# A hybrid trunk layer on one core: where four kinds of loads are issued, where two sums of weights are kept, and which engine adds the last residual columns

## The chip, the cores and the metric

The kernel runs on 1 core of one Trainium2 chip. The metric is the device time of one execution in microseconds (us), taken as the median over runs. One profiled execution gives the trace from which the rows below are quoted. The engines are TensorE (PE, with PEld for its weight loads), VectorE (DVE), ScalarE (ACT), GpSimd (POOL) and SyncE (SP, which here only issues DMAs).

## The reference, cut to what matters

```python
h = concat([meta, x])                                   # 272 rows of 2048
proj = rmsnorm(h, norm_mix) @ w_in                      # q, k, v, gates of 8 retention and 4 mLSTM heads
...
mix = concat([ret, hm]) @ w_out
h = h + mix
u = rmsnorm(h, norm_ffn)
up = causal_dwconv(u @ w_up, ffn_conv_w, ffn_conv_b)    # 11264 columns, kernel of 3
gate, val = split(up, [5632])
h = h + (silu(gate) * val) @ w_down                     # 5632 x 2048
return rmsnorm(h, norm_final)[16:]                      # 256 x 2048
```

All of it is float32. The change touches the first projection (its loads), the product with `w_down` (its loads and two sums of weight blocks) and the last residual sum ahead of the final norm.

## The kernel before, in words

Every float32 product is made of three products of 128-row blocks: weights w are split into whi (ACT rounds w, a CAST row) and wlo = w - whi (DVE), activations likewise into xh and xl, and PE sums xh*whi, xl*whi and xh*wlo in a bank. So each weight tile takes a DMA into the ring `wraw` (4 buffers), a cast on ACT, a subtraction on DVE, and then matmuls. The rings `whi` and `wlo` have 5 buffers each.

**The ramp** (the loop at L207). The first projection runs over 16 blocks k of the contracted axis while they still arrive: a DMA of hT (the input, 128x272 for each k) and one of w0 (128x320 for each k: two weight tiles and the gate columns), in portions of k = 0, 1, and then pairs. SP issues them, but for the first two w0 loads, which ACT issues, and `par`, the column of norm factors. ACT makes xh of each k and casts each w0 portion to whi; DVE makes wlo, the low part of the gate columns (the 64 columns of whi written at L227) and xl. Ahead of it PE multiplies a tile of ones WARM times (L199, two rows in the trace for each).

**The up projection and the down products**, in two halves of the 5632 columns. Each half has 11 down steps q of 256 columns of w_down, and there are two passes b = 0 and b = 2 over pairs of 512 output columns, with two row tiles tt. Steps 0, 4, 9 and 10 are plain: two loads of 512 KB in `wraw`, each cast and subtracted, and 24 matmuls (`product`, L814). The other steps are fast (`seven`, L832): seven products in place of eight. A fast step reads two DMAs into one of the two buffers `left` (they lie in hT; `turn` alternates), `kept` (256 KB, a sum made earlier and stored to DRAM) and three blocks of `wd7` (768 KB). From these DVE makes the sums ta (128x1024, L844) and tb (128x512, L845), and ta and tb each take a buffer of the ring `wraw` too. In half 1, pass 2, steps run in the order 0, 1, 4, 2, 7, 3, 5, 6 and then plain ones.

After the last fast step `share` combines four banks of PSUM and adds them to hn by DMAs that accumulate (hn<-x, issued by POOL); after the last step ACT copies the four banks of cs to x (L951), and these go to hn likewise. The banks are then written by the next pass.

**The tail** (L961). What the last four steps (`alone`) give to columns 1536 to 2047 of row tile 1 is summed apart, in two halves of 256 columns: PE, then DVE adds the bank to hn (L900), ACT squares it and sums (L694), then the chain for the final norm (`finish`: ACT Ln and Exp, DVE), and DVE and ACT scale hn (DVE L723 and L721, the latter with the gain `gfin`; columns that lie ready earlier are multiplied with the gain by POOL, L698) and store.

**What sets the order.** The framework orders the instructions of each engine by its own estimate of when they can run. `tc.issue_after(x)` keeps an instruction behind x in that order without a wait between engines of its own. Each engine and each DMA queue works in its order. SP waits at a DMA until its buffer is free, and all later DMAs of SP wait behind it.

## Time and profile before

| what | value |
|---|---|
| median of 3 runs | 1207.33 us (1207.29 to 1207.91) |
| profiled execution | 1207.7 us, its span 1205.9 us |
| TensorE clock granted, mean | 0.999 |
| PE busy | 1194.6 us, 99% of the span, 8956 matmul rows |
| DVE, ACT, POOL busy | 971.5, 709.5 and 162.8 us |
| moved by DMA | 263.27 MB, 218 GB/s over the span |

Times in the trace are counted from the first instruction. A row of the timeline is: start, duration, engine, line of the program, operation, written tile and read tiles, shape, how many in a row, and in brackets the idle time before it with what ended it. A matmul row's duration overlaps the next row's; the distance of two starts is what a matmul costs in a dense stretch.

### The profile page before, as it was taken

Reading aid. Unit: us, or ns where it says so; the run is one execution under the profiler, and the core shown is the slowest. Engines: PE = TensorE matmul, PEld = TensorE weight load, DVE = VectorE, ACT = ScalarE, POOL = GpSimd, SP = SyncE. Lnnn points to the kernel's source line nnn. Section 1 sums busy time; section 2 is a strip of 40 time slices with the busy share of each in tenths; the row PEclk is TensorE's granted clock in tenths of the full one; section 3 lists DMA queues with packets and bytes.
Section 4 is the critical chain, followed back from the end, with each engine's and each line's share of the span. In section 5 each row is a group of like instructions: output and inputs, shape, how many; then the busy total and the mean of one; then the engine's idle time right before and its main releaser. Section 6 shows DMA issues by size and latency. Waiting matters only on the chain.

```text
span 1205.9 us, 22794 instructions
## 1 busy us (share of the span) xinstructions
PE 1194.6 (99%) x8956; PEld 1151.2 (95%) x8956; DVE 971.5 (81%) x1444; ACT 709.5 (59%) x963; POOL 162.8 (14%) x223
## 2 busy tenths in 40 slices
PE   9999999999999999999999999999999999999997
PEld 9999999999999999999999998878999999998886
DVE  8968788766775966789889879897788778789897
ACT  8747656655656646555555557664555555556664
POOL 0100001111110311021122100202022112100232
PEclk9999999999999999999999999999999999999999
DMA  8765555666565965766766834959787777755956
GB/s 278 269 212 164 170 184 170 197 183 192 169 192 165 349 200 175 252 220 212 253 219 214 279 117 175 278 177 276 284 251 255 223 240 249 261 176 211 274 181 186
DMA packets 83004, 263.27 MB, mean 218 GB/s; under 512 B 14672, under 2 KB 18896, under 8 KB 82768
## 3 DMA queue, kind: packets, MB, share of 16 engines
q1 hardware_dynamic: 71952, 223.85, 57.0%
q0 software_dynamic: 10368, 37.11, 10.1%
q8 instruction: 70, 1.15, 0.4%
q10 hardware_dynamic: 576, 0.85, 0.2%
q14 instruction: 38, 0.31, 0.1%
HBM read 243.42 MB, written 11.27 MB: 211 GB/s over the span
## 4 chain that ended last, share of the span: by engine, by line
PE 96%; DMA 2%; DVE 1%; ACT 0%; issue 0%; SPq 0%; DVEq 0%; ACTq 0%
PE mmps L130 26%; PE mmps L131 25%; PE mmps L133 25%; PE atps L827 2%; PE atps L828 2%; PE atps L830 2%; PE mmps L860 2%; PE mmps L862 2%; PE mmps L859 2%; PE atps L862 1%; PE atps L860 1%; PE atps L859 1%; DMA hn<-x 1%; PE atps L379 1%; DMA hT<-in_wd 1%; PE atps L371 0%
## 5 line engine op out<-in xcount | busy, mean ns | idle before, releaser
L121 ACT CAST whi<-wraw 128x1024 fp32r<-128x1024 f32 x352 | 369.3, 1050 | 342.0 <-PE mmps L131 228.7
L123 DVE TENSOR_TENSOR wlo<-wraw,whi 128x1024 fp32r<-128x1024 f32 x352 | 432.3, 1230 | 72.5 <-ACT whi L121 70.0
L130 PE MATMUL mmps<-uh,whi 128*128 128x258 f32 x1408 | 346.1, 283 | 0.0
L131 PE MATMUL mmps<-ul,whi 128*128 128x258 f32 x1408 | 346.0, 283 | 0.0
L130 PEld LDWEIGHTS mmps<-uh,whi 128*128 128x128 f32 x1408 | 267.6, 190 | 0.1
L131 PEld LDWEIGHTS mmps<-ul,whi 128*128 128x128 f32 x1408 | 267.1, 190 | 0.1
L130 PE MATMUL mmps<-xh,whi 128*128 128x272 f32 (+2 forms) x864 | 219.8, 288 | 0.0
L131 PE MATMUL mmps<-xl,whi 128*128 128x272 f32 (+2 forms) x864 | 218.3, 286 | 0.0
L133 PE MATMUL mmps<-uh,wlo 128*128 128x258 f32 x1408 | 196.5, 282 | 0.0
L133 PEld LDWEIGHTS mmps<-uh,wlo 128*128 128x128 f32 x1408 | 179.9, 189 | 0.0
L131 PEld LDWEIGHTS mmps<-xl,whi 128*128 128x128 f32 x864 | 162.8, 188 | 0.0
L130 PEld LDWEIGHTS mmps<-xh,whi 128*128 128x128 f32 x864 | 162.5, 188 | 0.1
L133 PE MATMUL mmps<-xh,wlo 128*128 128x272 f32 (+2 forms) x864 | 126.7, 285 | 0.0
L133 PEld LDWEIGHTS mmps<-xh,wlo 128*128 128x128 f32 x864 | 114.2, 188 | 0.0
L680 DVE TENSOR_TENSOR cu<-mmps,rstd 128x258 f32<-128x258 f32 x88 | 37.4, 425 | 55.3 <-PE mmps L133 54.8
L764 ACT CAST whi<-hT 128x1024 fp32r<-128x1024 f32 x52 | 53.6, 1052 | 27.2 <-PE atps L828 7.3
L766 DVE TENSOR_TENSOR wlo<-hT,whi 128x1024 fp32r<-128x1024 f32 x52 | 62.1, 1220 | 4.9 <-ACT whi L764 3.7
L131 PE MATMUL mmps<-mixl,whi 128*128 128x258 f32 x256 | 63.0, 283 | 0.0
L130 PE MATMUL mmps<-mixh,whi 128*128 128x258 f32 x256 | 62.4, 282 | 0.0
L764 ACT CAST whi<-wraw 128x1024 fp32r<-128x1024 f32 (+1 forms) x52 | 43.0, 838 | 16.8 <-PE mmps L860 6.8
L766 DVE TENSOR_TENSOR wlo<-wraw,whi 128x1024 fp32r<-128x1024 f32 (+1 forms) x52 | 52.2, 1037 | 0.6 <-PE mmps L862 0.2
L827 PE MATMUL atps<-whi,mh 128*128 128x512 f32 (+1 forms) x132 | 50.9, 387 | 1.3 <-ACT whi L121 1.1
(280 smaller groups left out, 1700.1 us busy)
## 6 DMA issues: line engine op xcount, KB each, us to landing
wraw<-in_wu SPq DMA_DIRECT2D x176, 512.0 KB, 4.4
wraw<-in_wi SPq DMA_DIRECT2D x108, 512.0 KB, 4.1
hT<-in_wd SPq DMA_DIRECT2D x26, 768.0 KB, 4.7
wraw<-in_wd SPq DMA_DIRECT2D x36, 512.0 KB, 4.7
wraw<-in_wo SPq DMA_DIRECT2D x32, 512.0 KB, 4.2
x<-in_wd POOLq DMA_DIRECT2D x13, 768.0 KB, 7.0
hn<-x POOLq DMA_DIRECT2D x27, 256.0 KB, 7.9
hT<-kept SPq DMA_DIRECT2D x26, 256.0 KB, 2.9
```

The source lines that it names most:

```text
L121: nc.scalar.copy(hi, raw)
L123: nc.vector.tensor_tensor(out=lo, in0=raw, in1=hi.bitcast(F32), op=ALU.subtract)
L130: nc.tensor.matmul(ps, hi[:, k, :], xh(kk), start=kk == first, stop=False)
L131: nc.tensor.matmul(ps, hi[:, k, :], xl(kk), start=False, stop=False)
L133: nc.tensor.matmul(ps, lo[:, k, :], xh(kk), start=False, stop=kk == last)
L680: evacuated = nc.vector.tensor_tensor(out=u, in0=ps[:, :NQ], in1=rstd2, op=ALU.mult)
L764: copied = nc.scalar.copy(hi, x)
L766: return copied, nc.vector.tensor_tensor(out=lo, in0=x, in1=hi.bitcast(F32), op=ALU.subtract)
L827: nc.tensor.matmul(ps, ah[i], hi[:, i, cols], start=first and i == 0, stop=False)
L859: nc.tensor.matmul(o, sh[:, f, m, :], hi[:, i, :], start=begin, stop=False)
L860: nc.tensor.matmul(o, sl[:, f, m, :], hi[:, i, :], start=False, stop=False)
L862: nc.tensor.matmul(o, sh[:, f, m, :], lo[:, i, :], start=False, stop=end)
```

## The change

1. *Ramp.* ACT now issues the w0 loads of k = 0, 1 and 2-3 and `par`; SP issues hT and the later w0 loads. A copy of one column (rstd1<-ones) is made to stand behind these issues on ACT, and the casts are chained behind it. The w0 cast of k = 0 moves to DVE; the portion k = 2-3 is cast and subtracted one k at a time. The tile of ones is filled first, and WARM is 7.
2. *Sums out of the ring.* tb never takes a `wraw` buffer: in half 0 it lies in the tile `both` (which also takes gt and vt of the up projection), in half 1 ta and tb lie in the pool `more`, which begins when the pools of the up projection end. In half 0, ta stays in `wraw`.
3. *Down loads in order of use.* All of a half's loads for the down steps (plain, kept, wd7) are chained on SP in the order in which the program's steps use them.
4. *Last columns.* One matmul begins the bank pa1 of the last 256 columns, DVE adds the residual h to that bank (L998 of the new file) while PE sums pa0, PE then goes on in pa1, and ACT squares the bank itself. The last columns are scaled from the bank; columns 1536 to 1791 are multiplied with the gain by DVE in place of POOL.

```diff
...
 W0 = GW + 2 * P
-WARM = 8
+WARM = 7
...
-    nc.vector.memset(inv_dm, 1.0 / DM)
-    nc.vector.memset(epsc, EPS)
...
-    def load_w(src, shape, to=None):
+    def load_w(src, shape, to=None, after=None):
         nonlocal last_load
         raw = wpool.tile(shape, F32, name="wraw", bufs=4)
-        last_load = nc.sync.dma_start(raw, src)
+        with tc.issue_after(after.ins) if after else nullcontext():
+            last_load = nc.sync.dma_start(raw, src)
...
     nc.vector.memset(ones, 1.0)
+    nc.vector.memset(inv_dm, 1.0 / DM)
+    nc.vector.memset(epsc, EPS)
...
     with pool("sq", 1, side="right") as sqp:
-        for k0, k1 in [(0, 1), (1, 2)] + [(k, k + 2) for k in range(2, KT, 2)]:
+        chunks = [(0, 1), (1, 2)] + [(k, k + 2) for k in range(2, KT, 2)]
+        def ask(k0, k1):
+            nonlocal last_load
+            nc.sync.dma_start(hT[:, k0:k1, :], io["xT"][:, k0:k1, :])
+            raw = wpool.tile([P, 2, W0], F32, name="wraw", bufs=4)[:, : k1 - k0, :]
+            load = (nc.scalar if k0 < 4 else nc.sync).dma_start(raw, io["w0"][:, k0:k1, :])
+            if k0 == 0:
+                nc.scalar.dma_start(par[:, 0:KT], io["par"][:, 0:KT])
+            if k0 >= 4:
+                last_load = load
+            return raw, load
+        asked = {c: ask(*c) for c in chunks[:3]}
+        with tc.issue_after(asked[chunks[2]][1].ins):
+            copied = nc.scalar.copy(rstd1[:, 0:1], ones[:, 0:1])
+        for k0, k1 in chunks:
             n = k1 - k0
-            nc.sync.dma_start(hT[:, k0:k1, :], io["xT"][:, k0:k1, :])
-            if k0 == 0:
-                nc.sync.dma_start(par[:, 0:KT], io["par"][:, 0:KT])
-            raw = wpool.tile([P, 2, W0], F32, name="wraw", bufs=4)[:, :n, :]
-            queue = nc.scalar if k0 < 2 else nc.sync
-            load = queue.dma_start(raw, io["w0"][:, k0:k1, :])
-            if k0 >= 2:
-                last_load = load
-            for k in range(k0, k1):
-                nc.scalar.activation(xh[:, k, :], hT[:, k, :], AF.Copy, scale=pcol("gmix", k))
-                nc.vector.scalar_tensor_tensor(out=xl[:, k, :], in0=hT[:, k, :], scalar=pcol("gmix", k),
-                                               in1=xh[:, k, :].bitcast(F32), op0=ALU.mult, op1=ALU.subtract)
+            raw, _ = asked[k0, k1] if (k0, k1) in asked else ask(k0, k1)
             hi = wpool.tile([P, 2, W0 + GW], F32R, name="whi", bufs=5)[:, :n, :]
-            copied = nc.scalar.copy(hi[:, :, 0:W0], raw)
             lo = wpool.tile([P, 2, 2 * P], F32R, name="wlo", bufs=5)[:, :n, :]
-            nc.vector.tensor_tensor(out=lo, in0=raw[:, :, 0 : 2 * P], in1=hi[:, :, 0 : 2 * P].bitcast(F32), op=ALU.subtract)
-            parted = nc.vector.tensor_tensor(out=hi[:, :, W0:], in0=raw[:, :, 2 * P :], in1=hi[:, :, 2 * P : W0].bitcast(F32), op=ALU.subtract)
+            for c0, c1 in [(0, 1), (1, 2)][:n] if k0 < 4 else [(0, 2)]:
+                for k in range(k0 + c0, k0 + c1):
+                    with tc.issue_after(copied.ins) if k != 1 else nullcontext():
+                        nc.scalar.activation(xh[:, k, :], hT[:, k, :], AF.Copy, scale=pcol("gmix", k))
+                if k0 == 0:
+                    nc.vector.tensor_copy(hi[:, c0:c1, 0:W0], raw[:, c0:c1])
+                else:
+                    copied = nc.scalar.copy(hi[:, c0:c1, 0:W0], raw[:, c0:c1])
+                nc.vector.tensor_tensor(out=lo[:, c0:c1], in0=raw[:, c0:c1, 0 : 2 * P], in1=hi[:, c0:c1, 0 : 2 * P].bitcast(F32), op=ALU.subtract)
+                for k in range(k0 + c0, k0 + c1):
+                    with tc.issue_after(parted.ins) if k >= 2 else nullcontext():
+                        nc.vector.scalar_tensor_tensor(out=xl[:, k, :], in0=hT[:, k, :], scalar=pcol("gmix", k),
+                                                       in1=xh[:, k, :].bitcast(F32), op0=ALU.mult, op1=ALU.subtract)
+                parted = nc.vector.tensor_tensor(out=hi[:, c0:c1, W0:], in0=raw[:, c0:c1, 2 * P :], in1=hi[:, c0:c1, 2 * P : W0].bitcast(F32), op=ALU.subtract)
             for k in range(k0, k1):
...
-    def conv3(ps, f, name):
+    def conv3(ps, f, o):
...
         evacuated = nc.vector.tensor_tensor(out=u, in0=ps[:, :NQ], in1=rstd2, op=ALU.mult)
-        o = wk2.tile([P, SEQ], F32, name=name)
         nc.scalar.activation(o, u[:, 2:], AF.Identity, scale=pcol("fw", 3 * f + 2), bias=pcol("fb", f))
...
-    def finish(tt, n):
+    def finish(tt, n, end=None):
...
-        late = DM - 256 if n == 4 else DM - 512
+        late = DM - 512
...
             if c0 >= late:
-                nc.vector.scalar_tensor_tensor(out=h, in0=h, scalar=t, in1=gfin[:, c0:c1], op0=ALU.mult, op1=ALU.mult)
+                nc.vector.scalar_tensor_tensor(out=h, in0=h if end is None or c0 < DM - 256 else end, scalar=t, in1=gfin[:, c0:c1], op0=ALU.mult, op1=ALU.mult)
             else:
...
             nc.sync.dma_start(out[rows, c0:c1], hn[:, tt, c0:c1])
-        for c0, c1 in ((1536, late), (late, DM)):
-            if c0 < c1:
-                scale(c0, c1)
+        for c0, c1 in ((1536, DM),) if end is None else ((1536, 1792), (1792, DM)):
+            scale(c0, c1)
         nc.sync.dma_start(out[rows, 1536:], hn[:, tt, 1536:])
...
     left = hT.rearrange("p k t -> p (k t)")[:, 0:4096].rearrange("p (i a n) -> i p a n", i=2, a=4)
-    turn = 0
+    turn, asked = 0, None
...
-            gt = conv3(pair[0], j, "gt")
-            vt = conv3(pair[1], NF + j, "vt")
+            both = wk2.tile([P, 2, SEQ], F32, name="both")
+            gt = conv3(pair[0], j, both[:, 0, :])
+            vt = conv3(pair[1], NF + j, both[:, 1, :])
             nc.scalar.activation(gt, gt, AF.Silu)
...
-        def product(ps, tt, q, w, first=False, last=False, c0=0):
+        def product(ps, tt, q, w, first=False, last=False, c0=0, n0=0, n1=6, seed=False, seeded=False):
...
-            for i in range(2):
-                nc.tensor.matmul(ps, ah[i], hi[:, i, cols], start=first and i == 0, stop=False)
-                nc.tensor.matmul(ps, al[i], hi[:, i, cols], start=False, stop=False)
-            for i in range(2):
-                nc.tensor.matmul(ps, ah[i], lo[:, i, cols], start=False, stop=last and i == 1)
+            parts = [(a[i], hi, i) for i in range(2) for a in (ah, al)] + [(ah[i], lo, i) for i in range(2)]
+            for n, (a, m, i) in list(enumerate(parts))[n0:n1]:
+                nc.tensor.matmul(ps, a, m[:, i, cols], start=first and n == 0, stop=seed or last and n == 5, skip_group_check=seeded)
...
-            nonlocal turn
+            nonlocal turn, asked
...
-            nc.sync.dma_start(raw[:, 0, :], early[b, q])
-            nc.sync.dma_start(raw[:, 1:4, :], io["wd7"][b // 2, half * NQD + q][:, 1:4, :])
-            ta, tb = (wpool.tile([P, 2, 512], F32, name="wraw", bufs=4) for _ in range(2))
+            for to, src in ((raw[:, 0, :], early[b, q]), (raw[:, 1:4, :], io["wd7"][b // 2, half * NQD + q][:, 1:4, :])):
+                with tc.issue_after(asked.ins) if asked else nullcontext():
+                    asked = nc.sync.dma_start(to, src)
+            if half == 0:
+                ta = wpool.tile([P, 2, 512], F32, name="wraw", bufs=4)
+                tb = wk2.tile([P, 2, SEQ], F32, name="both").rearrange("p a t -> p (a t)")
+            else:
+                ta, tb = more.tile([P, 2, 512], F32, name="ta"), more.tile([P, 512], F32, name="tb")
             nc.vector.tensor_tensor(out=ta, in0=raw[:, 0:1, :].to_broadcast([P, 2, 512]), in1=raw[:, 1:3, :], op=ALU.subtract)
-            nc.vector.tensor_tensor(out=tb[:, 0, :], in0=raw[:, 3, :], in1=raw[:, 0, :], op=ALU.subtract)
+            nc.vector.tensor_tensor(out=tb, in0=raw[:, 3, :], in1=raw[:, 0, :], op=ALU.subtract)
             copied = None
...
                 (ta, ((S3, ps[1], first, last), (S1, ps[3], first, last))),
-                (tb[:, 0:1, :], ((A22, cs[1, 0], False, False),)),
+                (tb.rearrange("p (a n) -> p a n", a=1), ((A22, cs[1, 0], False, False),)),
             ):
...
-                reached = nc.gpsimd.tensor_tensor(out=junk[:, 0:1], in0=tb[:, 0, 0:1], in1=tb[:, 0, 0:1], op=ALU.add)
+                reached = nc.gpsimd.tensor_tensor(out=junk[:, 0:1], in0=tb[:, 0:1], in1=tb[:, 0:1], op=ALU.add)
...
         def load_step(b, q, to=wpool):
-            return load_w(io["wd"][b, half * NQD + q], [P, 2, 512], to)
+            nonlocal asked
+            w = load_w(io["wd"][b, half * NQD + q], [P, 2, 512], to, asked)
+            asked = last_load
+            return w
+        asked = None
...
             add(cs[1, 1], 1, c)
-            for i in range(2):
-                p = at.tile([P, 512], F32, name="atps")[:, 0:256]
-                for q in sorted(ws):
-                    product(p, 1, q, ws[q], q == alone[0], q == alone[-1], c0=i * 256)
-                add(p, 1, c + i * 256)
-                squares(1, 3 + i, c + i * 256, c + (i + 1) * 256)
-                if i == 0:
-                    times_gain(1, c, c + 256)
-                    gather(1, 4)
-            finish(1, 4)
+            qs = sorted(ws)
+            pa0, pa1 = (at.tile([P, 512], F32, name="atps")[:, 0:256] for _ in range(2))
+            h = hn[:, 1, c + 256 : DM]
+            product(pa1, 1, qs[0], ws[qs[0]], True, c0=256, n1=1, seed=True)
+            nc.vector.tensor_tensor(out=pa1, in0=pa1, in1=h, op=ALU.add)
+            for q in qs:
+                product(pa0, 1, q, ws[q], q == qs[0], q == qs[-1])
+            add(pa0, 1, c)
+            squares(1, 3, c, c + 256)
+            gather(1, 4)
+            for q in qs:
+                product(pa1, 1, q, ws[q], False, q == qs[-1], c0=256, n0=1 if q == qs[0] else 0, seeded=True)
+            nc.scalar.activation(junk[:, 0:256], pa1, AF.Square, scale=DM ** -0.5, accum_out=ss4[:, 1, 4:5])
+            finish(1, 4, pa1)
...
```

ACT at the start of the program, before (hT, w0 = in_w and par are inputs; xh<-hT,par is the activation split, whi<-wraw the weight cast):

```order
L215 DMA wraw<-in_w 128x320 x2
L224 ACT_TABLE_LOAD
L224 CAST whi<-wraw 128x320
L219 ACTIVATE xh<-hT,par 128x272
L224 CAST whi<-wraw 128x320
L219 ACTIVATE xh<-hT,par 128x272 x3
L224 CAST whi<-wraw 128x2x320
L219 ACTIVATE xh<-hT,par 128x272 x2
```

and now:

```order
L214 DMA wraw<-in_w 128x320
L216 DMA par<-in_par 128x16
L214 DMA wraw<-in_w 128x320
L214 DMA wraw<-in_w 128x640
L223 ACT_TABLE_LOAD
L223 COPY rstd_92<-ones 128x1
L232 ACTIVATE xh<-hT,par 128x272 x2
L236 CAST whi<-wraw 128x320
L232 ACTIVATE xh<-hT,par 128x272
L236 CAST whi<-wraw 128x320
L232 ACTIVATE xh<-hT,par 128x272
L236 CAST whi<-wraw 128x320
```

Four DMA issues stand ahead of the table load in place of two; the cast of the first portion is gone from ACT, and the 640-wide cast of k = 2-3 has become two of 320, each behind the xh of its k.

SP in half 0 from the last fast step of pass 0 on, before (kept_8 belongs to step 8 of pass 0, the later ones to pass 2; wraw<-in_wd are loads of plain steps):

```order
L840 DMA hT<-kept_8_6352 128x512
L841 DMA hT<-in_wd 128x1536
L840 DMA hT<-kept_1_6644 128x512
L841 DMA hT<-in_wd 128x1536
L118 DMA wraw<-in_wd 128x1024 x2
L840 DMA hT<-kept_2_6936 128x512
L841 DMA hT<-in_wd 128x1536
L118 DMA wraw<-in_wd 128x1024 x4
L840 DMA hT<-kept_3_7228 128x512
L841 DMA hT<-in_wd 128x1536
L840 DMA hT<-kept_5_7514 128x512
L841 DMA hT<-in_wd 128x1536
L118 DMA wraw<-in_wd 128x1024 x2
```

and now:

```order
L854 DMA hT<-kept_8_6352 128x512
L854 DMA hT<-in_wd 128x1536
L117 DMA wraw<-in_wd 128x1024 x6
L854 DMA hT<-kept_1_6642 128x512
L854 DMA hT<-in_wd 128x1536
L854 DMA hT<-kept_2_6932 128x512
L854 DMA hT<-in_wd 128x1536
L854 DMA hT<-kept_3_7222 128x512
L854 DMA hT<-in_wd 128x1536
L117 DMA wraw<-in_wd 128x1024 x2
L854 DMA hT<-kept_5_7506 128x512
```

Six plain loads (steps 9, 10 and the next pass's 0) now stand ahead of that pass's kept_1, and the two loads of its step 4 stand ahead of kept_5 and its wd7 blocks, not behind.

DVE at the end, before, from the add of the bank cs[1, 1] on (frt is the norm factor of a row; the 128x256 adds are those of the two halves of the last columns):

```order
L900 TENSOR_TENSOR hn<-atps,hn 128x512
L711 TENSOR_SCALAR frt<-ss_5848,rest 128x1
L900 TENSOR_TENSOR hn<-atps,hn 128x256
L713 SCALAR_TENSOR_TENSOR frt<-frt,fr_5852 128x1
L714 SCALAR_TENSOR_TENSOR frt<-frt,fr_5852 128x1
L723 TENSOR_SCALAR hn<-hn,frt 128x256
L723 TENSOR_SCALAR hn<-hn,frt 128x768
L721 SCALAR_TENSOR_TENSOR hn<-hn,frt,gfin 128x512
L703 TENSOR_REDUCE rest<-ss_5848 128x1
L704 TENSOR_SCALAR rest<-rest 128x1
L900 TENSOR_TENSOR hn<-atps,hn 128x256
L711 TENSOR_SCALAR frt<-ss_5848,rest 128x1
```

and now:

```order
L917 TENSOR_TENSOR hn<-atps,hn 128x512
L998 TENSOR_TENSOR atps<-atps,hn 128x256
L725 TENSOR_SCALAR frt<-ss_5851,rest 128x1
L727 SCALAR_TENSOR_TENSOR frt<-frt,fr_5855 128x1
L728 SCALAR_TENSOR_TENSOR frt<-frt,fr_5855 128x1
L737 TENSOR_SCALAR hn<-hn,frt 128x256
L737 TENSOR_SCALAR hn<-hn,frt 128x768
L735 SCALAR_TENSOR_TENSOR hn<-hn,frt,gfin 128x512
L917 TENSOR_TENSOR hn<-atps,hn 128x256
L717 TENSOR_REDUCE rest<-ss_5851 128x1
L718 TENSOR_SCALAR rest<-rest 128x1
L725 TENSOR_SCALAR frt<-ss_5851,rest 128x1
```

The add into the bank (atps<-atps,hn) stands early, the add of the other half has moved behind the three scalings of row tile 0, and no add is left behind PE's last matmul.

## The prediction

> **What bounds the kernel now.** I read the page's head and its chain that ended last first, then PE's waits, then the timeline at each place where PE waits or where the change moves something.
>
> ```profile
> PE 1194.6 (99%) x8956; PEld 1151.2 (95%) x8956; DVE 971.5 (81%) x1444; ACT 709.5 (59%) x963; POOL 162.8 (14%) x223
> PE 96%; DMA 2%; DVE 1%; ACT 0%; issue 0%; SPq 0%; DVEq 0%; ACTq 0%
> PE atps L827 <- ACT whi L121: 1.1, 2, 0.7
> PE atps L130 <- ACT whi L224: 0.7, 1, 0.7
> PE atps L827 <- ACT x L951: 0.2, 1, 0.2
> ```
>
> PE is the bound nearly everywhere, and the change leaves the number of its matmuls alone, but for one warming matmul that lies ahead of the first data. So the change can give back only what PE waits, plus what stands ahead of PE's first and behind its last matmul. The three rows of waits are short, yet they are the places that the change touches. What a wait costs is read from the distance of two starts on PE less the normal one, since a matmul after a pause also starts slower. The profiled execution took 1207.7 us against a median of 1207.33, so my sum is made against 1207.7 and then lowered by 0.4. A difference of 0.2%, 2.4 us, is about what a measurement of this kernel tells from none.
>
> **The ramp: 0.75 us less.**
>
> ```profile
> 1.21 3.79 PE L199 MATMUL atps<-ones 128*128 128x128 f32 x16 [1.21 <-DVE ones L171]
> 4.89 0.39 PE L130 MATMUL atps<-xh,whi 128*128 128x272 f32 x1
> 5.12 0.29 PE L130 MATMUL mmps<-xh,whi 128*128 128x262 f32 x1
> 5.25 0.29 PE L235 MATMUL atps<-xh,whi 128*128 128x272 f32 x1
> 7.05 0.29 PE L236 MATMUL atps<-xl,whi 128*64 128x272 f32 x1
> 8.02 0.39 PE L130 MATMUL atps<-xh,whi 128*128 128x272 f32 x1 [0.68 <-ACT whi L224]
> 2.12 4.15 DMA hT<-in_xT
> 6.29 0.94 ACT L219 ACTIVATE xh<-hT,par 128x272 fp32r<-128x272 f32 x2 [0.69 <-DMA hT<-in_xT]
> 7.24 0.72 ACT L224 CAST whi<-wraw 128x640 fp32r<-128x640 f32 x1
> 4.74 0.44 ACT L224 CAST whi<-wraw 128x320 fp32r<-128x320 f32 x1
> 2.60 0.43 SPq L215 DMA_DIRECT2D wraw<-in_w  x1
> GB/s 0 0 0 0 0 11 96 112 290 389 338 389 345 221 62 116 198 322 377 376 359 377 390 369 407 392 384 393 355 354 389 418 412 405 405 404 417 393 419 393
> ```
>
> Between 7.05 and 8.02 PE does one matmul, whose normal distance is 0.13 us (5.12 to 5.25). So 0.84 us is lost there. PE waits for a chain: the hT pair of k = 2-3, issued at 2.12 as SP's fourth DMA, lands at 6.27; ACT splits both, 0.94 us; then it casts both in one piece, 0.72 us. The last line (40 slices of the first 12 us) shows the transfers dip near 4.5 us, between two waves of issues, and then run full.
>
> After the change hT of 2-3 is SP's third issue and w0 of 2-3 ACT's fourth; both come some 0.45 us earlier (one issue, the 0.43 of L215), and w0 of 2-3 no longer queues behind hT. I take its landing as 6.6 in place of 7.2. The cast of k = 2 alone then takes 0.44 and ends near 7.1, with xh of k = 2 already made. PE has k = 0 and 1 done near 6.9, so k = 2 begins some 0.9 us earlier than 8.02. The portion 4-5 still waits for ACT's two splits and 640-wide cast, which end near 9.5; PE would want it near 9.1. That gives 0.2 to 0.4 back, and the first real matmul comes 0.15 earlier, since the cast of k = 0 moves beside ACT's work to DVE. Net 0.75. The ends: 0.2, if the loads land hardly earlier; 1.2, if the portion 4-5 comes as early as 2-3. The two further issues on ACT (0.43 each) put its table load 0.9 later; I take that as hidden, because PE's first real matmul at 4.89 waited for loads that the line of transfers shows under way until near 4 us. At worst it eats the 0.15.
>
> The Trainium skill, page "DMA: Bandwidth & Descriptors", section "Issuing engines are not separate DMA queues", speaks against much of this term: DMAs from several engines run on the same 16 DMA engines, and issuing from several saves only the issue time. By that alone the term would be the 0.45 us of one issue. The full GB/s slices from 5 us on agree; the dip near 4.5 us does not.
>
> **Half 0, pass 2: 1.6 us less.**
>
> ```profile
> 778.91 6.88 DMA hT<-in_wd
> 787.74 1.15 DVE wlo L766
> 788.90 3.52 DMA wraw<-in_wd
> 792.54 0.63 PE L862 MATMUL mmps<-wlo,sh 128*128 128x512 f32 x2
> 793.62 0.50 PE L827 MATMUL atps<-whi,mh 128*128 128x512 f32 x1 [0.45 <-ACT whi L121]
> 793.96 0.39 PE L828 MATMUL atps<-whi,ml 128*128 128x512 f32 x1
> 814.57 4.94 SPq L118 DMA_DIRECT2D wraw<-in_wd  x4
> 817.99 0.63 PE L862 MATMUL mmps<-wlo,sh 128*128 128x512 f32 x2
> 819.27 0.51 PE L827 MATMUL atps<-whi,mh 128*128 128x512 f32 x1 [0.65 <-ACT whi L121]
> ```
>
> The first three rows are the chain that ended last, in order of time: wd7 of step 3 lands at 785.8, a subtraction frees a ring buffer at 788.9, only then is the load of step 4 issued. It lands at 792.4, ACT casts it, PE starts at 793.62. A matmul costs 0.23 in dense work (1.07 for the run of four at 1138.96 below against 0.63 for this run of two), so the next start after 792.54 was due at 793.0: 0.62 lost, and 0.11 more because the first matmul after the pause takes 0.34. Step 9 repeats it: due 818.45, started 819.27, 0.82 and 0.12. Together 1.67.
>
> Now a fast step holds one ring buffer, not two, and SP asks for step 4 ahead of kept_5. Its buffers are free after step 0's subtractions, so the loads go out right behind wd7 of step 3, near 780 to 781, and land by some 789; ACT reaches the cast after step 3's, near 791, ahead of 793.0. Step 9, asked for at 814.57 so far, moves ahead of the pass's last fast steps' buffers likewise, and needs 1 us only. I take 1.6.
>
> What is queued behind: SP now issues six plain loads ahead of kept_1, so kept_1, kept_2 and their wd7 blocks go out later than before, when the accumulating DMAs of `share` run.
>
> ```profile
> 772.92 2.25 ACT L951 COPY x<-atps 128x512 f32<-128x512 f32 x4
> 785.89 2.00 ACT L764 CAST whi<-hT 128x1024 fp32r<-128x1024 f32 x2 [2.62 <-PE atps L862]
> 788.17 0.39 PE L859 MATMUL atps<-whi,sh 128*128 128x512 f32 x1
> ```
>
> The four copies wait for accumulations that read the same x. PE needs them one by one, 1.37 us apart (six matmuls of 0.23), and a copy takes 0.56 (2.25 for four), so the fourth has some 2.4 us in hand. The two late pairs carry 2.0 MB, of which I let half meet the accumulations: at the 380 GB/s above that is 2.6 us less what overlaps. Behind that, kept_3 goes out up to 2 us later. If its wd7 then still took 6.88, it would land at 787.8, and a cast of 1.0 would end at 788.8 where PE began step 3 at 788.17. PE now puts two matmuls ahead of that one, which leaves 0.2 over. Cost taken as 0, since the queue is emptier by then; bounds 0 and 1.5 (all 2.0 MB ahead of the accumulations would be 5.3 us against 2.4 in hand; half of that overrun). A gain beyond the two waits is excluded, since PE is dense elsewhere.
>
> **Half 1: 0.4 us less.**
>
> ```profile
> 1138.60 1.05 ACT L121 CAST whi<-wraw 128x1024 fp32r<-128x1024 f32 x1 [1.53 <-DMA wraw<-in_wd]
> 1138.96 1.07 PE L830 MATMUL atps<-wlo,mh 128*128 128x512 f32 x4
> 1140.19 0.50 PE L827 MATMUL atps<-whi,mh 128*128 128x512 f32 x1 [0.16 <-ACT x L951]
> 1088.06 1.22 DVE L844 TENSOR_TENSOR wraw<-hT 128x1024 f32<-128x1024 f32 x1
> 1089.53 0.68 DVE L845 TENSOR_TENSOR wraw<-hT 128x512 f32<-128x512 f32 x1
> 1089.19 0.42 DVE L766 TENSOR_TENSOR ml<-gt,mh 128x256 fp32r<-128x256 f32 x1
> 1093.40 0.62 PE L862 MATMUL mmps<-wlo,sh 128*128 128x512 f32 x2
> ```
>
> PE was due at 1138.96 + 4 x 0.23 = 1139.87 and began at 1140.19, because the copy of the bank stood on ACT behind a cast whose load landed at 1138.5. With ta and tb out of the ring this load goes out earlier, ahead of the accumulations; it needs to land 0.3 us earlier only, and the copy then follows PE directly: 0.32 and 0.1 gone.
>
> The price is at the half's start. ta and tb can be written only when the up projection's pools have ended, behind ml<-gt; that subtraction moves up to near 1088, and DVE then does ta, tb, ta, tb (1.22, 0.68, 1.22, 0.68) and wlo of ta, 1.2 less overlaps, ending near 1092.8; PE needs it at 1093.40. Cost 0 with 0.6 us in hand; bounds 0 and 1.
>
> **The tail: 0.3 us less.**
>
> ```profile
> 1197.92 0.41 DVE L900 TENSOR_TENSOR hn<-atps,hn 128x256 f32<-128x256 f32 x1
> 1198.37 0.42 ACT L694 ACTIVATE junk<-hn 128x256 f32<-128x256 f32 x1 [1.91 <-DVE hn L900]
> 1199.92 0.35 DVE hn L723
> 1200.98 0.48 DVE L721 SCALAR_TENSOR_TENSOR hn<-hn,frt,gfin 128x256 f32<-128x256 f32 x1
> ```
>
> The add at 1197.92 leaves the end: ACT can square the bank when the add would have begun, 0.45 us earlier. The last scaling of 256 columns with the gain (0.48) replaces one without (0.35): 0.13 back. Net 0.3. The other half's add, its square and the gather must fit into 1196.9 to 1198.2 behind row tile 0's scalings, and they do only if those are not slower than before; if they are, 0.4 of it goes. Bounds 0.35 less and 0.1 more.
>
> **Sum.** 0.75 + 1.6 + 0.4 + 0.3 = 3.05 less: 1204.65 beside the profiled 1207.7, and 1204.3 beside the median, which I predict.
>
> **The rivals.**
> - *New waits take half of it.* The prefetches meet the accumulations (1.5), or the half-1 start runs over (1), or the ramp is bound by bandwidth (0.55 of its 0.75 missing). For it: slacks of 0.6 to 1.2 us, read off loads that take 4 to 7 us. Against it: PE's order gives each cast its own slack. With 1.5 us lost: 1205.9, no measurable change.
> - *The clock rises later.* Seven warming matmuls (3.79 us times 14/16) begun 0.15 earlier end near 4.4, and the first real one comes near 4.7, so PE pauses where it was busy before. Before, starts are 0.23 apart at 4.89 and 0.13 from 5.12 on: the step came 3.8 us after the first warming matmul. If a pause restarts that time, k = 0 and 1 run at half pace, and some 1.7 us is lost: 1206.0. The Trainium skill, page "TensorE: Matmul & The Clock Gate", section "Part 1: The HAM clock gate", says that the clock follows a free-running window of about 3.4 us, whose place varies from run to run; by that the pause need not cost anything, and this rival would show in some runs alone. No row here decides it.
> - *Slower.* At the start of half 1, DVE's four sums are ahead of every wlo and wait for the pools' end. If that wait ends late, nothing covers it: each us beyond the 0.6 in hand is a us on PE. It decides from 5.4 us beyond on (3.0 gained, 2.4 to be seen), that is if DVE starts near 1094, about when PE would have passed step 1. For it: `more` waits for readers on all engines, the gain's load among them. Against it: the last reader is the subtraction near 1088. Price then 1207.3 + 2.4 and up, 1210.
> - *Nothing of the order of loads matters*, since the ring stays short in half 0 (ta still in it): the 1.6 stays, 1205.9. Against it: the chain's row at 787.74 names the subtraction of tb's group as what frees the buffer.
>
> **How the numbers follow.** All four terms: 0.52. Half lost to new waits or to bandwidth: 0.24. Late clock: 0.11. Ring still short: 0.05. Slower: 0.08. The first case's own range is 1203.4 to 1205.0; the next three lie at 1205.9 to 1206.5. So the range is 1203.3 to 1206.9, which leaves out the slower case and the outer parts of the others. Faster by over 0.2% means below 1204.9: most of the first case and a little of the second, 0.53. Within 0.2%: 0.39. Slower: 0.08.
>
> **What would show it.** In the changed profile: k = 2 on PE near 7.1 and no wait for a whi of over 0.4 us before 10 us; no wait of PE for ACT's whi near 793 and 819, and none for the copy near 1140; ACT's last square directly behind PE's last matmul. A wait of PE near 780 to 791, at 1090 to 1096, or half-paced starts after 5 us would prove me wrong.

## The result and the profile after

The changed kernel takes 1224.36 us (1223.48 to 1227.46, 4 runs) against 1207.55 us (1207.29 to 1207.91) for the one before: ratio 1.0144, 95% interval 1.0125 to 1.0162. It is slower by 16.8 us where 3.0 us less was forecast. The profiled execution took 1224.72 us, its span 1222.9 us.

The page's first line and the waits of PE after the change (who waited, for what; us in total, times, longest):

```profile
PE 1201.1 (98%) x8954; PEld 1155.4 (94%) x8954; DVE 970.4 (79%) x1447; ACT 704.5 (58%) x963; POOL 168.6 (14%) x222
PE atps L879 <- DVE wlo L779: 5.3, 1, 5.3
PE atps L842 <- ACT x L972: 4.1, 5, 1.7
PE atps L132 <- DVE wlo L122: 1.7, 1, 1.7
PE atps L842 <- DVE hn L917: 0.7, 2, 0.5
```

The two waits for whi that carried the largest term of the forecast are gone, as is the one for k = 2 in the ramp (whether the change removed them is asked further below). In their place stand others, six times as long. To see what each place costs I paired PE's matmuls of the two traces by number, the warming ones left out, and took the difference of their starts (after less before):

| up to | difference, us | this part alone | forecast |
|---|---|---|---|
| 12 us, the ramp | +1.15 | +1.15 | -0.75 |
| 31 us, the second projection | +4.64 | +3.49 | 0 |
| 825 us, half 0 with its pass 2 | +6.43 | +1.79 | -1.6 |
| 1181 us, half 1 | +15.40 | +8.97 | -0.4 |
| PE's last matmul | +17.13 | +1.73 | 0 |
| the end of the span | +17.0 | -0.1 | -0.3 |

**Ramp.** PE's timeline after:

```profile
4.97 0.60 PE L129 MATMUL atps<-xh,whi 128*128 128x272 f32 x1 [0.55 <-ACT xh L232]
8.71 0.43 PE L129 MATMUL atps<-xh,whi 128*128 128x272 f32 x1
10.05 0.43 PE L250 MATMUL atps<-xh,whi 128*128 128x272 f32 x1
27.26 1.96 PE L132 MATMUL atps<-xh,wlo 128*128 128x272 f32 x8 [1.74 <-DVE wlo L122]
```

The first real matmul comes at 4.97, not at 4.7; starts are 0.22 apart until 10.3, so k = 2 begins at 8.71 (before: 8.02) without a wait. Its whi had been ready since 7.93, by ACT's row:

```profile
7.47 0.46 ACT L236 CAST whi<-wraw 128x320 fp32r<-128x320 f32 x1 [1.29 <-DMA wraw<-in_w]
```

At 27.26 PE waits for a wlo, which it did not before. DVE's rows there, after and then before:

```profile
23.55 0.43 DVE L299 COPY g<-atps 4x272 f32<-4x272 f32 x1 [2.23 <-PE atps L253]
23.91 1.27 DVE L270 TENSOR_TENSOR sum<-sum,turns 128x1088 f32<-128x1088 f32 x1
26.00 2.34 DVE L122 TENSOR_TENSOR wlo<-wraw,whi 128x1024 fp32r<-128x1024 f32 x2
```

```profile
22.42 0.43 DVE L284 COPY g<-atps 4x272 f32<-4x272 f32 x1
22.78 2.34 DVE L123 TENSOR_TENSOR wlo<-wraw,whi 128x1024 fp32r<-128x1024 f32 x2
```

The changed order puts three other instructions ahead of the two wlo. In this execution the clock also fell to half pace from 27.3 to 30.8, some 1.6 us more.

**Half 0, pass 2.** The copies of the banks to x on ACT, the four sums of `share` on DVE, and the busy time of 8 us each (columns: window, length, busy time of PE, PEld, DVE, ACT, POOL with counts, clock, DMA share, GB/s), all after:

```profile
770.90 0.58 ACT L901 COPY x<-mmps 128x512 f32<-128x512 f32 x1
780.97 0.58 ACT L972 COPY x<-atps 128x512 f32<-128x512 f32 x1 [3.33 <-DMA hn<-x]
783.13 0.59 ACT L972 COPY x<-atps 128x512 f32<-128x512 f32 x1 [1.58 <-DMA hn<-x]
785.21 0.58 ACT L972 COPY x<-atps 128x512 f32<-128x512 f32 x1 [1.48 <-DMA hn<-x]
```

```profile
771.51 0.69 DVE L903 TENSOR_TENSOR x<-mmps,x 128x512 f32<-128x512 f32 x1 [1.07 <-ACT x L901]
773.25 0.68 DVE L904 TENSOR_TENSOR x<-mmps,x 128x512 f32<-128x512 f32 x1
778.33 0.68 DVE L906 TENSOR_TENSOR x<-x,mmps 128x512 f32<-128x512 f32 x1
778.93 0.68 DVE L912 TENSOR_TENSOR x<-x,mmps 128x512 f32<-128x512 f32 x1
```

```profile
760.00:768.00 8.00, 8.00 (x36) 6.57 (x35) 8.00 (x10) 4.82 (x5) 0.00 (x0) 1.00 0.29 79
776.00:784.00 8.00, 5.76 (x24) 4.12 (x24) 5.50 (x7) 2.71 (x4) 3.04 (x4) 1.00 1.08 271
```

And before, the first and last sum and the same windows:

```profile
764.25 0.68 DVE L886 TENSOR_TENSOR x<-mmps,x 128x512 f32<-128x512 f32 x1
766.43 0.68 DVE L895 TENSOR_TENSOR x<-x,mmps 128x512 f32<-128x512 f32 x1
```

```profile
760.00:768.00 8.00, 8.00 (x36) 6.57 (x35) 6.80 (x9) 4.19 (x5) 2.74 (x4) 1.00 1.01 347
776.00:784.00 8.00, 8.00 (x36) 6.56 (x35) 6.47 (x7) 6.21 (x8) 1.31 (x2) 1.00 1.05 239
```

Two things differ. The sums end at 779.6 instead of 767.1, 7.9 us late beyond the 4.6 that the kernel was late already; they used to stand together, and now stand among the subtractions of six plain loads. And from 760 to 768 the DMA engines moved 79 GB/s where they moved 347 (196 GB/s in the window 4.6 us later, the same place of the kernel): with SP in order of use, kept and wd7 of steps 1 and 2 waited behind plain loads that waited for ring buffers, and came with all the rest once the accumulations had begun.

**Half 1.** PE's waits, and the DVE row behind which the last one stands:

```profile
1149.92 0.50 PE L842 MATMUL atps<-whi,mh 128*128 128x512 f32 x1 [0.74 <-ACT x L972]
1152.31 0.50 PE L842 MATMUL atps<-whi,mh 128*128 128x512 f32 x1 [0.73 <-ACT x L972]
1161.05 1.22 PE L879 MATMUL atps<-wlo,sh 128*128 128x512 f32 x2 [5.26 <-DVE wlo L779]
```

```profile
1158.03 1.22 DVE L861 TENSOR_TENSOR ta<-hT 128x1024 f32<-128x1024 f32 x1 [8.58 <-DMA hT<-in_wd]
```

The wd7 block of step 2, issued at 1141.63, landed at 1157.94: 16.3 us for 768 KB, against 6.9 in the row at 778.91 of the forecast. DVE waited for it in front of every later wlo.

**Tail.** SP's last loads after and before:

```profile
1194.37 2.60 SPq L117 DMA_DIRECT2D wraw<-in_wd  x3
```

```profile
1171.96 11.19 SPq L118 DMA_DIRECT2D wraw<-in_wd  x7
```

Before, the last of these loads was issued at 1182.8; now at 1196.6. PE waits for DVE's adds (0.7) and the rest is late in the same way.

### The profile page after: what moved, and what is told of

It reads as the page before. It is cut to its first block, busy times and chain, and to the rows that moved or that the text cites. A ratio compares the mean times of both kernels' runs of the same rounds, so it can differ in the third digit from the quotient of the medians.

```text
span 1222.9 us, 22787 instructions
## 1 busy us (share of the span) xinstructions
PE 1201.1 (98%) x8954; PEld 1155.4 (94%) x8954; DVE 970.4 (79%) x1447; ACT 704.5 (58%) x963; POOL 168.6 (14%) x222
## 3 DMA queue, kind: packets, MB, share of 16 engines
q8 instruction: 70, 1.15, 0.4%
## 5 line engine op out<-in xcount | busy, mean ns | idle before, releaser
L698 DVE SCALAR_TENSOR_TENSOR both<-cu,par,both 128x256 f32<-128x256 f32 x176 | 84.8, 482 | 6.4 <-ACT both L696 4.2
L696 ACT ACTIVATE both<-cu,par 128x256 f32<-128x256 f32 x88 | 53.0, 602 | 43.5 <-DVE cu L695 30.7
```

What stands on the lines that cost most here:

```text
L696: nc.scalar.activation(o, u[:, 2:], AF.Identity, scale=pcol("fw", 3 * f + 2), bias=pcol("fb", f))
L698: nc.vector.scalar_tensor_tensor(out=o, in0=u[:, j : j + SEQ], scalar=pcol("fw", 3 * f + j), in1=o, op0=ALU.mult, op1=ALU.add)
```

## The experiments

Ratios are against the kernel before, run on the same chip. From e5 on the theories are: T1, the order of use makes loads meet the accumulating DMAs; T2, the new places of ta and tb do it; T3, formed after e7, share's sums stand late on DVE, so accumulations go out late, and the copies of the banks, which reuse the sums' tiles, keep PE waiting; T4, its rival, loads and accumulations collide whatever DVE does.

### The ramp: e1 to e4, e15

e1 is the kernel before with the ramp's hunks of the change alone (queues, split casts, WARM = 7).

> The ramp part of the change alone (loads on two queues, tile of ones first, WARM 7); loads, sums and tail as before. Theory: the whole offset that the changed kernel has by 31 us, 4.6 us, belongs to this part: near 1212.0, with PE at half pace from 5 to 10.5 us, a PE wait of 1.9 us near 25 us for the wlo of the next tile, and half pace again to 31 us. Rival: the wait near 25 us comes from the later parts (other orders of DVE), then about 1208.7 and no such wait.

1214.15 us against 1207.34, ratio 1.0060 (1.0041 to 1.0079). Its profile has the wait for wlo at 27 us again (1.7), starts 0.22 apart until 9.5, and waits of 1.7 for a copy and 1.3 for casts in the down products. The second stretch at half pace, which was expected too, is not in it, so that stretch does not follow from the wait each time.

e2 adds to e1 that DVE takes the second projection's first wlo ahead of the gates:

```diff
-            with tc.issue_after(parted.ins), tc.high_priority():
+            with tc.issue_after((parted if k == 4 else v0_lo).ins), tc.high_priority():
...
-        nc.vector.tensor_copy(o, gates_ps[g : g + MH, :T])
+        with tc.issue_after(v0_lo.ins):
+            nc.vector.tensor_copy(o, gates_ps[g : g + MH, :T])
```

> As the ramp alone, but on DVE the two wlo of the first whole tile stand ahead of the copies of the gate columns and of the third sum of squares. Theory: the wait near 25 us is DVE's order, and the second stretch at half pace follows from that wait: both go, 3.5 us less than the ramp alone, near 1208.5. Rival: the second half-paced stretch has a cause of its own (it follows the late first rise): only the 1.9 us go, near 1210.2.

1211.49 us, 1.0027 (1.0015 to 1.0039). The wait at 27 us is gone and with it 2.7 us. The second half-paced stretch was not in e1, so e2 can't test what causes it. The ramp's part still costs 4 by the medians, 3.3 by the ratio, more than either forecast.

e3 is the kernel before with WARM = 7 and nothing else; e4 is e2 with WARM = 9.

> The kernel before with 7 warming matmuls in place of 8, nothing else. Theory: a pause ahead of the first real matmul delays the step of the clock: half pace to about 10 us, 1 to 2 us slower, near 1209. Rival: the clock's step has a phase of its own: 1207.5, half pace ends near 5 us as before.

> As the ramp with wlo first, with 9 warming matmuls, so that they end near 4.9 us and PE does not pause. Theory: full pace from about 5 us, and the ramp's own gain shows: near 1206.8. Rival (phase of its own): like the run with 7, near 1208.5.

e3: 1207.27 us, 1.0000 (0.9990 to 1.0009). e4: 1211.33 us, 1.0026 (1.0014 to 1.0039). A warming matmul more or less changes nothing that can be measured here. In e3's profile the full pace came at 6.8 us only, and the time was the same, since PE would have waited for k = 2 anyway.

e15 is e2 with the loads on the queues of before, and everything else of the ramp's new order:

```diff
-            load = (nc.scalar if k0 < 4 else nc.sync).dma_start(raw, ...)
-                nc.scalar.dma_start(par[:, 0:KT], ...)
+            load = (nc.scalar if k0 < 2 else nc.sync).dma_start(raw, ...)
+                nc.sync.dma_start(par[:, 0:KT], ...)
```

> The ramp of e2 (DVE's order at the second projection mended) with its loads on the queues of before: par and w0 of 2-3 on SP; split casts, 7 warming matmuls and the rest of the ramp's new order stay. If the two queues cost e2's 4 us: 1206.5 to 1208. If the new order of the ramp's work costs them: 1210 to 1212.5.

1208.79 us against 1207.73, 1.0008 (0.9997 to 1.0018). So of e2's 3.3 us (by the ratios) some 2.3 belong to the two queues. This is close to the noise: the two intervals just overlap, and e15 lies between its two forecasts. In e15 k = 2 begins earlier than before the change, although the pace rose late (at 5.9):

```profile
7.63 0.40 PE L129 MATMUL atps<-xh,whi 128*128 128x272 f32 x1 [0.22 <-ACT whi L236]
```

The DMA records say why. After the change w0 of 2-3 was issued at 2.15 (before: 2.60) and landed at 7.45 (7.21); w0 of k = 1, now third on ACT behind par, landed at 5.28 (4.33). Earlier came hT of 2-3 (5.09 in place of 6.27), hT of 4-5 (7.23 in place of 7.94) and the loads behind them (w0 of 4-5: 8.12 in place of 8.76), which are needed later. In e2 the two w0 loads landed at 8.11 and 6.62, in e15 at 7.10 and 4.17. By the page "DMA: Bandwidth & Descriptors" of the Trainium skill, section "Issuing engines are not separate DMA queues", several issuers save the issue time only; the trace agrees: w0 of 2-3 was issued 0.45 us earlier and landed 0.24 later. That the loads brought forward on the other queue delayed it is inferred from e15, where both w0 loads land as before. Of e2's loss, only 0.9 us lies ahead of 12 us in its profile (the longest of its runs); why the rest appears as late loads near 770 us in e1, e2 and e4, and less in e15, stays open.

### One part at a time: e5 to e8

e5 is the changed kernel without the order of use (the lines below, against the changed kernel); e6 is the kernel before with that order alone.

```diff
-                with tc.issue_after(asked.ins) if asked else nullcontext():
+                with nullcontext():
                     asked = nc.sync.dma_start(to, src)
...
-            w = load_w(io["wd"][b, half * NQD + q], [P, 2, 512], to, asked)
+            w = load_w(io["wd"][b, half * NQD + q], [P, 2, 512], to)
```

> The changed kernel without the order of use between the loads of the down projection's steps (each load goes out where its buffer and the scheduler let it); ramp, sums out of the ring and tail as changed. T1 (the order of use sends the kept blocks and wd7 of steps 1 and 2 behind six plain loads, so that they meet the accumulating DMAs): the 3.1 us before step 4 of half 0 and most of the 8.6 us in half 1 go, the ramp's 4 to 7 us stay: 1209 to 1213. T2 (the new places of ta and tb, and the scheduler's new order with them, do it): stays at 1222 to 1226.

> The kernel before with the order of use between the down projection's loads as its only edit; ta and tb still take ring buffers, ramp and tail as before. T1: the accumulations are met as in the changed kernel, and a load that waits for a ring buffer now also holds the kept blocks behind it: 10 us slower or more, 1217 to 1225. T2: the order alone costs little, 1206 to 1209.

e5: 1222.41 us against 1206.95, 1.0130 (1.0102 to 1.0158). e6: 1221.18 us, 1.0115 (1.0097 to 1.0134). Each expectation holds for one theory and fails for the other: the order costs 14 us by itself, and without it the changed kernel is as slow as with it. In e6's trace the sums of `share` end at 769.6, only 2.5 us later than before, so its loss is not theirs. So T1 is one sufficient cause, and there must be a second.

e7 is the kernel before with ta and tb out of the ring alone, e8 with the changed end alone.

> The kernel before with ta and tb out of the ring as the only edit (with both, the tile that gt and vt and tb share). T1: the two stalls of step 4 and step 9 in half 0 go, nothing is put in their place: 1205.3 to 1207, 1 to 2 us less than before. T2: 5 us slower or more, 1212 to 1216, with waits of PE in half 0 near 780 and in half 1.

> The kernel before with the changed end alone (row tile 1's last 256 columns get the residual in the bank, and their square and scaling read the bank). T1 (the end lost its gain because the last loads were late and the add of the other 256 columns stood behind row tile 0's scalings on DVE): with the loads on time as before, 0 to 0.3 us less, 1207.0 to 1207.4. T2 (the end's own order of instructions costs more than it saves): 0.5 to 1 us slower, 1208.

e7: 1225.71 us, 1.0149 (1.0134 to 1.0164), with 10.9 us of waits for the copies. T1 had forecast 1205.3 to 1207: it falls as the only cause. The ring's part, from which the forecast had its largest gain, costs 18 us alone. e8: 1206.24 us, 0.9996 (0.9987 to 1.0005): the tail's 0.3 us is there in sign, too small to be told from none. In e8's profile the span ends 8.0 us behind PE's last start, before 8.5.

### The place of the sums: e9 to e12

In e7's trace the sums ran from 769.1 to 777.2, among the wlo of plain loads. e9 (changed kernel), e10 (e7) and e12 (all but the ramp) put them back: the copy of p1, the four sums ahead of the third plain load's cast and wlo, and of ta and tb.

```diff
+        held[2] += 1
+        g = held if held[0] and held[2] > 2 else None
+        with tc.issue_after(g[0].ins) if g else nullcontext():
             nc.scalar.copy(hi, raw)
+        with tc.issue_after(g[1].ins) if g else nullcontext():
             nc.vector.tensor_tensor(out=lo, in0=raw, ...)
...
-            nc.scalar.copy(x1, p1)
+            held[0] = None if final else nc.scalar.copy(x1, p1)
...
-            nc.vector.tensor_tensor(out=x5, in0=x7, in1=p5, op=ALU.subtract)
+            held[1] = nc.vector.tensor_tensor(out=x5, in0=x7, in1=p5, op=ALU.subtract)
+            held[2] = 0
```

e11 does the reverse in the kernel before: its loads and ring are untouched, and the sums are written after the third and fourth plain load and kept behind their wlo.

```diff
+            owed[:] = [None, None, sums1, sums2]
...
+            if owed:
+                sums = owed.pop(0)
+                if sums:
+                    with tc.issue_after(last_lo.ins):
+                        sums()
```

> The changed kernel, with one order put back on DVE and ACT: at the end of a column pass the copy of p1 and share's four sums stand ahead of the cast and of the subtraction of the third plain load, as before the change. T3 (the sums stood behind wlo subtractions that wait for loads, so the accumulating DMAs went out 6 to 14 us late, and the bank copies that reuse their tiles kept PE waiting): PE's waits for the copies go, 9 to 12 us less than the changed kernel, 1212 to 1216; what is left over before is the ramp's 4 to 7. T4 (the loads and the accumulations share the DMA engines, whatever DVE's order): 1219 to 1224.

> The kernel of e7 (ta and tb out of the ring, nothing else) with the same order of copy and sums put back. T3: the 18 us of e7 go and the two stalls of half 0 stay away: 1205 to 1207.5. T4: 1215 or more.

> The kernel before, loads and ring unchanged; only the four sums of share are written after the third, fourth plain load, so that DVE does them behind those loads' subtractions (the last two behind the sixth), as the changed kernel does. T3: the accumulations of halves 0 and 1 go out some 8 us later, PE waits 4 to 8 us at each of the two places: 1214 to 1222. T4: 1206 to 1209.

> The changed kernel without the ramp's part, with copy and sums put back as in e9. T3: no wait for the copies, the stalls of steps 4 and 9 gone, the end a little shorter: 1204.5 to 1207. T4: 1212 or more. If it lies between, the order of use has a price of its own, to be read from PE's waits near 785 and 1150.

e11: 1219.25 us against 1206.55, 1.0093 (1.0076 to 1.0109), as T3 forecast; by the paired starts PE loses 6.0 us at the copies of half 0 and 6.7 at those of half 1. The chain that ended last, in order of time, shows the whole of T3 in this kernel:

```profile
762.73 7.08 DMA wraw<-in_wd
...
770.50 1.22 DVE wlo L123
771.72 0.61 DVE x L890
...
772.63 3.22 DMA hn<-x
...
777.16 4.14 DMA hn<-x
...
781.38 0.59 ACT x L966
...
782.02 0.80 PE atps L827
```

A load, the subtraction that waits for it, the sum behind it on DVE, its accumulation, the next one, the copy that needs its tile, and PE.

e10: 1212.76 us, 1.0048 (1.0033 to 1.0063): some 12 of e7's 18 us go, as T3 has it, but the forecast of 1205 to 1207.5 is missed. Its profile (1210.11, the shortest of its runs) has PE 0.4 us behind the kernel before at the end and nothing lost up to 1160; then 2.5 us go in waits for wlo at 1172 and 1178, and 2 us behind PE, where DVE's adds of the last banks stand late again. What its longer runs lose besides can't be read from it; e16 below, with half 1's sums back in the ring and the changed end, does not have this loss.

e9: 1221.61 us, 1.0110 (1.0091 to 1.0128): T3's forecast of 1212 to 1216 fails, T4's 1219 to 1224 holds. e12: 1216.68 us, 1.0074 (1.0053 to 1.0096), beyond the 1212 that spoke for T4. e12's sums are in place (765.3 to 768.1), and the loads in order of use are late all the same, as in e6; e12's windows and its DVE row:

```profile
756.00:764.00 8.00, 8.00 (x37) 6.56 (x36) 8.00 (x9) 3.75 (x4) 0.00 (x0) 1.00 0.20 77
772.00:780.00 8.00, 6.61 (x27) 4.47 (x25) 3.06 (x3) 2.37 (x4) 1.72 (x2) 1.00 1.08 312
```

```profile
781.41 1.23 DVE L853 TENSOR_TENSOR wraw<-hT 128x1024 f32<-128x1024 f32 x1 [3.31 <-DMA hT<-in_wd]
```

The DMA engines are 20% busy, then over 100%; wd7 of step 2 takes 14.1 us.

### Without the accumulations: e13, e14

The one line of `onto`, which issues hn<-x, is left out of the changed kernel (e13) and of the one before (e14); the partial sums are missing in the output. The order on DVE and SP stays that of each kernel.

```diff
-            nc.gpsimd.dma_start(block(tt, b), x, accum_op=ALU.add)
+            pass
```

> The changed kernel without the accumulating DMAs hn<-x (the partial sums are left out of the output); the order on DVE is that of the changed kernel. T3 (late sums cost only because the accumulations behind them are late and hold tiles and DMA engines): all waits of PE in halves 0 and 1 go, 11 to 13 us less than the changed kernel; what is left over e14 is the ramp's 4 to 6: 1210 to 1213. If late sums also hold PE's banks by themselves, or the loads in order of use are late without any accumulation: 1216 or more.

> The kernel before without the accumulating DMAs, as the control of e13. The stalls of step 4 and step 9 come from the ring and stay: 1205 to 1207, 0 to 2 us less than before.

e13: 1208.55 us against 1207.73, 1.0006 (0.9996 to 1.0015). e14: 1205.84 us, 0.9983 (0.9973 to 0.9992). e13 is 15.8 us shorter than the changed kernel, more than the 11 to 13 expected, and 2.7 longer than e14: of the changed kernel's 16.8 us some 14 hang on the accumulations. Late sums and loads in order of use cost PE nothing by themselves in half 0 and half 1 (e13's paired starts are 4.6 us behind at 31 us and 4.0 at 1181): both work through the accumulations. An accumulation takes time of the DMA engines and also holds the tile that a later copy needs; e13 leaves out both, so it does not divide the two. e14 was expected to keep the stalls of steps 4 and 9, and neither is in its profile, though its ring is as before. What e13 still waits for is the ramp's:

```profile
PE atps L132 <- DVE wlo L122: 1.7, 1, 1.7
PE atps L200 <- DVE ones L170: 1.1, 1, 1.1
PE atps L129 <- ACT xh L232: 0.6, 1, 0.6
```

### The parts that should help: e16 to e18

e16 and e18 are one kernel: before, with ta in the ring and tb in `both` in half 0, two ring buffers as before in half 1, the sums first as in e10, and the changed end. e17 is the same without the sums first. The lines of half 1 against e10:

```diff
-                ta, tb = more.tile([P, 2, 512], F32, name="ta"), more.tile([P, 512], F32, name="tb")
+                ta, tb2 = (wpool.tile([P, 2, 512], F32, name="wraw", bufs=4) for _ in range(2))
+                tb = tb2[:, 0, :]
```

> The kernel before with ta and tb out of the ring in half 0 alone (half 1 keeps two ring buffers for each step), copy and sums first as in e10, and the changed end. If e10's loss lies in half 1 and the end: the two stalls go and the end saves 0.3 to 0.7, 1204.5 to 1206. If it lies in half 0's loads meeting the accumulations: 1209 to 1212.

> The kernel of e16 without the order of copy and sums, so that at the end of half 0's first pass share's sums stand among six subtractions of plain loads again (in half 1 they stay ahead by themselves). T3: the wait of half 0 is back alone, some 6 us over e16: 1210 to 1214. If the order of the sums does not matter there: 1205 to 1207.

> The kernel of e16 again, beside e17, with more rounds. Expected as e16 measured: 1.0 to 2.5 us less than before, 1204.8 to 1206.3.

e16: 1205.96 us against 1207.73, 0.9982 (0.9972 to 0.9993). e18, on another chip: 1207.62 us against 1207.05, 1.0002 (0.9994 to 1.0011). e17, beside e18: 1210.93 us, 1.0035 (1.0024 to 1.0047). The place of the sums is worth 3.3 us in half 0 alone (6 expected). That e16's kernel is faster than the one before is not shown: the gain of one chip was missing on the other, though both profiles have PE ending earlier (by 0.7 and 2.0 us) with the two stalls gone. (In e3, with the ring as before, PE also ends 1.35 us earlier without the two stalls, and the median is the same as before.) No version here that computes the whole output is shown to beat the kernel before.

## Why the prediction was wrong

*Half 0, pass 2.* The mechanism of the gain was right as far as the loads go: with tb out of the ring and the sums in place, step 4's load goes out at 781.1 (e16) and 779.8 (e18) in place of 788.9 and lands by 788.1, as forecast. (In the changed kernel it went out only at 790.1, behind wd7 of step 3, which had to wait for its own buffer.) Its size was not: the step "Together 1.67" took the waits of one execution for a fixed price. In e3, where the ring is as before, step 4's load landed at 791.86 in place of 792.42, and PE went from step 3 into step 4 without a wait:

```profile
792.96 0.62 PE L862 MATMUL mmps<-wlo,sh 128*128 128x512 f32 x2
793.42 0.39 PE L827 MATMUL atps<-whi,mh 128*128 128x512 f32 x1
```

At step 9 it lost 0.1 us, at the copy near 1140 nothing. The 1.67 us lie within the spread of single runs of the kernel before (1205.47 to 1210.81 in the runs beside e1 to e4), and no run shows the forecast gain. That the stalls are gone in the changed kernel proves nothing either, since PE came there 7.5 us late.

The step that turned the sign is "Cost taken as 0, since the queue is emptier by then; bounds 0 and 1.5". I followed the moved loads on SP and looked at the slack of the copies, and never asked what the change does to the order on DVE and ACT. There the sums of `share`, on which the accumulations hang, went from a place ahead of the third plain load to one among six (e11, and e7 against e10: 11 to 12 us by the ratios). The moved loads themselves were priced too low as well: the order of use alone costs 14 us (e6). I counted the accumulations as if they met the loads at 380 GB/s; they take twice as long (below). The upper bound of 1.5 us was drawn from the fourth copy's 2.4 us in hand with an unchanged start of the accumulations; beyond the kernel's own 4.6 us they started up to 8 us later.

*Half 1.* The wait for the copy at 1140 went (it is not in e3 either), and at 1149.92 and 1152.31 two others came, then the one at 1161.05. The step that failed is the same, applied to the accumulations of half 1; the forecast priced only the half's start (ta, tb and the pools), and there, at 1090 to 1096, PE waits nowhere, as forecast.

*Ramp.* Three steps failed. "I take its landing as 6.6 in place of 7.2": it landed at 7.45, so whi of k = 2 was ready at 7.93 and the gain of 0.9 us was gone. I had the rule against it in hand and still took a gain from it. In the changed kernel's trace this alone would have cost nothing, since k = 2 began at 8.02 before; in e9, at full pace from 5.2, the load landed at 7.83, PE waited 1.01 us for the cast and began k = 2 at 8.36. The second is the late clock, a rival at 1.7 us with a chance of 0.11: at half pace PE was done with k = 0 and 1 only at 8.71, and that, not the load, set the start of k = 2 (0.7 us late, 1.15 by 12 us). The third is the DVE order at 26 us (1.9 us, and in this execution a half-paced stretch behind it), which lay outside the places that I compared.

*Tail.* e8's profile ends 0.5 us sooner behind PE's last start, which fits the reason; its time (0.9996) does not tell 0.3 us from none. In the changed kernel the last loads and adds were late.

*The rivals.* None of the four gives the 16.8 us. "New waits take half of it" named the right meeting, loads and accumulations, at 1.5 us in place of some 14. The late clock did occur and cost some 1 us by 12 us. A rise at 6.8 (e3) or 7.2 (e11) in place of 5.1 was free (0.2 us behind and 0.1 ahead at 12 us), because at full pace PE would have waited for k = 2 anyway; the rise at 10.3 was not. The slow rival put its price at half 1's start, where nothing was lost. Of the signs that I named against me, two came: waits between 781 and 786 and half-paced starts after 5 us.

## What to carry to other kernels

When tiles change their pool or ring, a scheduler reorders engines that the change does not mention: compare the order on every engine at each instruction that starts a long chain (here a sum that feeds an accumulating DMA), and price the chain from its first link. A wait of less than 1 us in one profile is not yet a price: look for it in a second execution of the same kernel before a change is to earn it. Before loads are moved, ask what they meet when they go earlier or bunch. A plain in-order queue in order of use is not neutral: one load that waits for a buffer holds everything behind it, while the DMA engines idle (20% busy in e12 where the kernel before has 100%).

## What the runs showed of the hardware

An accumulating DMA (x added into hn, issued by POOL) cost about twice a load's DMA time for each byte. From the DMA view of the kernel before, 760 to 785 us (queue: packets, MB, share of 16 engines; q1 carries loads, q0 the eight hn<-x):

```profile
q1 hardware_dynamic: 1309, 4.61, 53.2%
q0 software_dynamic: 1152, 2.10, 49.7%
```

That is 2.9 us of all 16 engines for 1 MB loaded (0.532 x 25 / 4.61) and 5.9 us for 1 MB accumulated; the eight accumulations of one pass fill the engines for 12.4 us, and a 768 KB load among them took up to 16.3 us. The size of the packets is not the reason: in the trace's packet records of the same window the median packet of 2048 bytes took 178 ns on q0 and 84 ns on q1.

The rise of PE's clock comes at different times in executions that begin alike: full pace at 5.1 us in the kernel before and at 7.2 in e11, both with eight warming matmuls from 1.21 and no pause; at 5.2 in e9, 9.5 in e1 and 10.3 in the changed kernel, all three with seven and a pause of 0.5. The page "TensorE: Matmul & The Clock Gate" of the Trainium skill, section "Part 1: The HAM clock gate", has a free-running window of about 3.4 us and a rise that varies by 0.5 us to either side with where in it the first matmul falls. The spread of 2.1 us without a pause lies within one window, but is more than those 0.5 us. The one of 5.1 us with a pause is more than one window, and no run here settles why.
